# A table with a place in time for every step, in a decoder step of two layers on one core

## The chip, the core and the metric

The kernel runs on one core of a Trainium2 chip. A core has engines that run side by side, each its own queue of instructions strictly in order: TensorE (PE, matmuls and transposes), VectorE (DVE), ScalarE (ACT), GpSimd (POOL) and SyncE (SP, which here issues most DMAs). They tell each other by semaphores when something is ready. Matmuls write to PSUM, which has eight banks; everything else lies in SBUF. The metric is the device time of one execution in microseconds; lower is better.

## The reference

One inference step of a hybrid decoder with two layers, for a prompt of 512 tokens and for 8 samples of 8 tokens each. D = 1024, so 576 token columns in all.

```python
# layer 0: gated DeltaNet mixer
h = rms_norm(x) * (1 + scale) + shift                # scale, shift, gate = c @ ada_w + b
qkv, z, beta, a = split(h @ w_in)
qkv = silu(causal_conv(qkv))
o, state = gated_delta_rule(q, k, v, g, beta, s0)    # chunked, with a triangular inverse per chunk
x = x + gate * ((rms_norm(o) * silu(z)) @ w_out)
# shared keys and values
k, v = split(modulate(x) @ w_kv)                     # k: RMS norm per head, partial rotary
# layer 1: differential attention
q, z = split(modulate(x) @ w_in)
k_all, v_all = [cache pages, k], [cache pages, v]    # samples: 1024 past positions in 8 pages
p = softmax(q1 @ k1) - lam * softmax(q2 @ k2)
x = x + gate * ((rms_norm(p @ v_all) * silu(z)) @ w_out)
```

## The kernel before

**Products.** The large products keep 8 x 128 rows of weights and stream the 576 columns in two halves of 288. For float32 accuracy weights and activations are each split into a high and a low part (hi, lo: `whi`, `wlo`, `hhi`, `hlo`), and a product is three matmuls: hi x hi, hi x lo, lo x hi. 105 chunks of 128 output rows are made so. All other matmuls are plain float32.

**Stages.** `Opening` (0 to about 48 us) loads x and the first modulation weights, makes the norm and the first two chunks. The first layer follows (class `Weave`, to about 620 us): 8 groups of 2 heads, each with convolution, transposes, scaled keys, a triangular inverse in small blocks (`tinv_pe`: 32x32 and 64x64 parts of the PE array), the chain over 4 chunks, and the samples' states. 24 units of modulation weights (`ada_units`) run beside them with 128x32 parts of the array. Then the second layer (class `Second`): output projection of layer 0, second norm, q, k, v and gate products, the samples' attention over cache pages, the prompt's attention, the output projection.

**The order.** Nothing is ordered by hand. Each piece of work is a generator that yields its next step: the engine ("E" PE, "L" PE for small blocks, "A" ACT, "D" and "S" DVE, "P" and "Q" POOL, None for none), a cost in microseconds and conditions (names of results, `Room` for a free buffer). `drive` keeps a clock per engine, and at each turn runs the step that can start soonest; among those that can start at the same time, the one with the smallest key. The order in which steps are run is the order of the instructions in each engine's queue (`pin`, `woven`). The key before is a rank per work plus an entry of `NUDGE`, by the work's name and count: 188 entries for the first layer, 72 for the second. Once a work has its rank, all its steps have it.

The planner's prices: `matmul`, `turn` and, in the second layer, `change` add to a step's cost; a change of the array's shape costs 0.2 us back to 128x128 and 0.115 otherwise. `ready` adds `PAD` when a PE step follows another engine. DMA transfers get a landing time from `transfers`, with a margin per kind in `SLACK`. Where PE would be idle for over `GAP` = 0.6 us, `fill` issues dummy bf16 matmuls of 105 ns by its account (L368; in the opening L535), in the first layer alone; in the second it returns 0.

**The start.** In `body`, four records of matmuls on zeros (L3227), then a memset of part of `hhi` on POOL (L3228) and eight matmuls on it (L3230) run before `Opening`.

**Samples' attention.** `Sample2.keys` (one per sample b) builds block queries `qs`, and for each half of the sample's 8 key pages takes one of two `px` banks and makes the scores of 4 pages: 8 matmuls per page in 128x32 parts, for b >= `PB` = 3 four pages in one step (`BURST`), else two. ACT copies a half to SBUF (L2642). When both are done `softmax` starts: a PE step of its own makes the scores with the new keys in another `px` bank, 8 matmuls with 64 columns (all samples' new keys, of which 8 are this sample's), DVE adds the mask to the 8 columns that count, and max, exp and transposes follow. `values` makes the product with the value pages.

## Time and profile before

| | us |
|---|---|
| median of 3 runs | 1127.67 |
| lowest, highest | 1126.29, 1132.82 |
| the profiled execution, its own time | 1126.22 |
| its span, first to last instruction | 1124.5 |
| granted TensorE clock, mean | 0.995 |
| idle time of PE before steps that waited for POOL WF L868, ACT hhi L2785, DMA wlo<-wall, DVE hlo L1959 | 2.4, 2.2, 2.0, 2.0 |
| DMA, mean | 213 GB/s |

The profile is of one execution. Times within it are counted from the first instruction. A row of a group gives line, engine, operation, tiles (out<-in), shape and count, then busy time, mean duration and the idle time before it. A row of the timeline gives start, duration, engine, line, operation, tiles, shape and count. Matmuls overlap each other, so what one costs is read from start to start, not from its duration; a float32 matmul leaves two records, a transpose or a 288-column product one. Shapes like 128*32 are the rows and columns of the array in use. L347 and L2034 are the helpers that issue matmuls in the first and the second layer, so tiles tell what is what: pp and pq hold large products, px<-pg the scores with cache pages, px<-kT,qs those with the new keys, po<-pg the products with value pages, sc<-kT,qT the prompt's scores, pa<-araw modulation units.

### The profile page before, as it was taken

How to read it: one execution, taken by the hardware profiler on the slowest of the kernel's cores; microseconds unless marked ns; L12 is line 12 of the kernel's file. 1: busy time of each engine (PE TensorE's matmuls, PEld its weight loads, DVE VectorE, ACT ScalarE, POOL GpSimd, SP SyncE). 2: the span in 40 equal slices, each digit the busy share in tenths (PEclk: the TensorE clock that was granted, in tenths of full speed). 3: DMA queues.
4: the chain of work that ended last, by engine and by line, in shares of the span. 5: the costliest groups of instructions: out<-in, count | busy, mean ns of one | idle time of the engine just before them, and what ended most of it. 6: DMA issues, size and time to landing. Idle time of an engine off the chain costs nothing.

```text
span 1124.5 us, 32457 instructions
## 1 busy us (share of the span) xinstructions
PE 1098.5 (98%) x12641; PEld 1025.7 (91%) x12641; DVE 702.9 (63%) x1839; ACT 678.2 (60%) x1829; POOL 453.9 (40%) x769
## 2 busy tenths in 40 slices
PE   8989999999999999999999999999999999999998
PEld 6789999999999999999999899899898888888988
DVE  3576986878767887677835659574333457654421
ACT  3476867778596876868564334685444567655510
POOL 3434434344334433343124441589862233323421
PEclk8999999999999999999999999999999999999999
DMA  9685776584767766586696849413849888888742
GB/s 364 194 221 138 176 187 188 150 238 115 199 159 209 193 186 154 119 258 193 205 289 204 317 139 352 167 64 109 297 147 315 301 306 287 299 307 296 264 137 92
DMA packets 87643, 239.97 MB, mean 213 GB/s; under 512 B 14450, under 2 KB 28658, under 8 KB 87490
## 3 DMA queue, kind: packets, MB, share of 16 engines
q1 hardware_dynamic: 71938, 181.27, 46.6%
q0 software_dynamic: 15552, 56.63, 22.2%
q8 instruction: 100, 1.64, 0.6%
q14 instruction: 53, 0.43, 0.1%
HBM read 212.02 MB, written 25.84 MB: 212 GB/s over the span
## 4 chain that ended last, share of the span: by engine, by line
PE 88%; DVE 4%; DMA 3%; POOL 2%; issue 1%; ACT 1%; SPq 0%; POOLq 0%; DVEq 0%; ACTq 0%
PE pp L347 28%; PE pp L2034 14%; PE pq L2034 7%; PE pc L347 6%; PE px L2034 4%; PE po L2034 4%; PE pa L347 3%; PE sc L2034 3%; PE pt L2039 3%; PE pt L347 3%; PE ps L347 2%; PE pv L2034 2%; PE pt L2034 2%; PE pt L361 2%; PE pp L368 1%
## 5 line engine op out<-in xcount | busy, mean ns | idle before, releaser
L347 PE MATMUL pp<-hlo,whi 128*128 128x288 f32 x592 | 170.7, 310 | 0.0
L347 PE MATMUL pp<-hhi,whi 128*128 128x288 f32 x592 | 162.0, 295 | 0.0
L2136 POOL TENSOR_TENSOR wlo<-wraw,whi 128x512 fp32r<-128x512 f32 x78 | 104.2, 1350 | 110.8 <-ACT whi L2130 96.5
L2034 PE MATMUL pp<-hhi,whi 128*128 128x288 f32 x432 | 131.6, 305 | 0.0
L2034 PE MATMUL pp<-hlo,whi 128*128 128x288 f32 x432 | 127.3, 295 | 2.7 <-DVE hlo L1959 2.0
L2034 PE MATMUL pp<-hhi,wlo 128*128 128x288 f32 x432 | 126.8, 299 | 0.0
L347 PE MATMUL pp<-hhi,wraw 128*128 128x288 f32 x576 | 122.5, 298 | 0.0
L347 PEld LDWEIGHTS pp<-hlo,whi 128*128 128x128 f32 x592 | 111.5, 188 | 1.7 <-issue 1.0
L347 PEld LDWEIGHTS pp<-hhi,whi 128*128 128x128 f32 x592 | 111.5, 188 | 0.7
L347 PE MATMUL pp<-hhi,wlo 128*128 128x288 f32 x592 | 103.1, 303 | 2.0 <-DMA wlo<-wall 2.0
L347 PEld LDWEIGHTS pp<-hhi,wraw 128*128 128x128 f32 x576 | 93.6, 188 | 1.0 <-issue 0.2
L347 PEld LDWEIGHTS pp<-hhi,wlo 128*128 128x128 f32 x592 | 85.1, 188 | 3.6 <-DMA wlo<-wall 2.3
L1218 DVE SCALAR_TENSOR_TENSOR y<-u,vec,y 128x600 f32<-128x600 f32 x96 | 82.8, 868 | 5.0 <-ACT y L1215 4.0
L2034 PEld LDWEIGHTS pp<-hlo,whi 128*128 128x128 f32 x432 | 81.5, 189 | 3.1 <-DVE hlo L1959 2.2
L347 PE MATMUL pp<-hlo,wraw 128*128 128x288 f32 x288 | 84.1, 314 | 0.1
L2034 PEld LDWEIGHTS pp<-hhi,whi 128*128 128x128 f32 x432 | 81.4, 188 | 2.1 <-issue 1.8
L2034 PEld LDWEIGHTS pp<-hhi,wlo 128*128 128x128 f32 x432 | 81.8, 191 | 0.0
L2593 POOL COPY pg<-ptt 1x1 int32<-1x1 int32 x128 | 26.4, 217 | 122.4 <-PE po L2034 55.9
L1012 POOL DMA_DIRECT2D wlo<-wall x36 | 32.1, 893 | 94.3 <-ACT wlo L1007 65.9
L2130 ACT CAST whi<-wraw 128x1024 fp32r<-128x1024 f32 x45 | 47.2, 1048 | 35.7 <-PE px L2034 12.9
L2034 PE MATMUL pq<-hhi,whi 128*128 128x288 f32 x192 | 62.1, 324 | 0.2 <-ACT vch L2350 0.2
L2034 PE MATMUL pq<-hlo,whi 128*128 128x288 f32 x192 | 56.6, 295 | 0.0
(507 smaller groups left out, 3113.9 us busy)
## 6 DMA issues: line engine op xcount, KB each, us to landing
pg<-ck SPq DMA_DIRECT2D x64, 512.0 KB, 5.3
pg<-cv SPq DMA_DIRECT2D x64, 512.0 KB, 5.6
wraw<-wall SPq DMA_DIRECT2D x49, 512.0 KB, 4.3
wraw<-wall POOLq DMA_DIRECT2D x36, 512.0 KB, 7.0
whi<-wall POOLq DMA_DIRECT2D x36, 512.0 KB, 5.9
wlo<-wall POOLq DMA_DIRECT2D x36, 512.0 KB, 7.0
araw<-ada SPq DMA_DIRECT2D x24, 512.0 KB, 6.2
araw<-ada SPq DMA_DIRECT2D x8, 1024.0 KB, 13.5
```

Source lines behind the costliest of these rows:

```text
L347: return self.K.nc.tensor.matmul(**kw)
L361: return self.K.nc.tensor.transpose(**kw)
L368: self.K.nc.tensor.matmul(out=self.banks[0][:, HT:512].rearrange("p (a b) -> p a b", b=32), lhsT=self.K.ident[:, 0:64].bitcast(BF16), rhs= ...
L1012: K.nc.gpsimd.dma_start(out=lo[:], in_=src, accum_op=ALU.add)
L1218: nc.vector.scalar_tensor_tensor(out=y[:, :YW], in0=u[:, j:j + YW], scalar=cw[j], in1=y[:, :YW], op0=ALU.mult, op1=ALU.add)
L2034: return self.K.nc.tensor.matmul(**kw)
L2039: return self.K.nc.tensor.transpose(**kw)
L2130: nc.scalar.copy(out=hi[:], in_=raw[:])
L2136: (nc.vector if shared else nc.gpsimd).tensor_sub(out=lo[:, q:q + 4], in0=raw[:, q:q + 4], in1=hi[:, q:q + 4].bitcast(F32))
L2593: nc.gpsimd.tensor_copy(out=e, in_=P.ptt[0:1, i:i + 1])
```

## The change

1. `NUDGE` goes. `PLAN` holds, for each work, a place in time for each of its steps: 3435 steps of the first layer, 2274 of the second. A work is found by its name and a checksum of its path (the works that added it, with counts). The key of a step is its place; where there is none, `LAST` = 10000 plus the old rank. `Opening` has no table.
2. The planner's prices change: one rule for both layers, shape changes `ENTER` 0.23 (from 128x128), `ACROSS` 0.137 (between smaller shapes), `EXIT` 0.1 (back); small matmuls are counted per position in the array, the slowest position telling; `PAD` 0.5 to 0.1; `SLACK` of "w" 1.0 to 2.0 and of "x" 6.0 to 3.5 in the first layer.
3. For samples b >= `PB` the scores with the new keys are made in the step of the second half's pages, which takes both `px` banks and waits for all new keys. For all samples these matmuls have 8 columns instead of 64.
4. The memset of `hhi` and the eight matmuls behind it go from the start.
5. Opening a later tile of a group waits for ("cs0", g); the condition for choosing a free bank for gate products moves into `pick`.

```diff
-NUDGE = {
...
+PLAN = {
+    "Weave": """ada_loads 766088 14922 -11238 7264 2040 951 1320 2419 -702 1511 4123 2612 47 3127 3708 -1357 4500 3316 3411 975 1512 -624 -338 281 2685
...
+def planned(cls):
+    out = {}
+    for line in PLAN.get(cls, "").split("\n"):
+        name, i, *steps = line.split() or ("", 0)
+        at, out[name, int(i)] = 0, []
+        for t in steps:
+            at += int(t)
+            out[name, int(i)].append(at / 100)
+    return out
...
     def matmul(self, **kw):
...
+        if wide:
+            self.cost += 0.16 if rhs.dtype == BF16 else max(0.062, n * 0.00046)
+        elif shape == (128, 128):
+            self.cost += max(0.224, n * 0.00175)
         else:
-            cost = max(0.224, n * 0.00168)
...
+            at = kw.get("tile_position")
+            lane = self.lanes.get(at, 0.0) + max(0.062, n * 0.00182)
+            self.lanes[at] = lane
+            self.cost += max(0.0, lane - self.lane)
+            self.lane = max(lane, self.lane)
...
+    def turn(self, shape):
         if shape != self.shape:
-            self.cost += 0.2 if shape == (128, 128) else 0.115
-        elif kind == 2 and self.kind != 2:
-            self.cost += TURN
-        self.shape, self.kind = shape, kind
+            self.cost += EXIT if shape == (128, 128) else ENTER if self.shape == (128, 128) else ACROSS
...
+    def key(self, v):
+        return v[5][v[6]] if v[6] < len(v[5]) else LAST + v[0]
...
-PAD = 0.5
+PAD = 0.1
...
         for pair in range(4 // many):
             ids = [b * NPG + 4 * half + many * pair + i for i in range(many)]
-            yield "E", None, *[("kpage", i) for i in ids], *((Room("px"),) if pair == 0 else ())
+            joined = b >= PB and half
+            yield ("E", None, *[("kpage", i) for i in ids], *((Room("px"),) if pair == 0 else ()),
+                   *((Room("px"), *[("k", h) for h in range(8)]) if joined else ()))
...
+            if joined:
+                self.new(qs, W.took[1])
...
+    def new(self, qs, xr):
...
-                K.mm(out=pn[32 * j:32 * j + 32, 0:64], lhsT=qs[:, h, :], rhs=P.kT[:, h, SEQ:],
+                K.mm(out=pn[32 * j:32 * j + 32, 0:8], lhsT=qs[:, h, :], rhs=W.P.kT[:, h, SEQ + 8 * b:SEQ + 8 * b + 8],
                      start=(hh == 0), stop=(hh == 1), tile_position=(0, 32 * j))
...
+        if b < PB:
+            yield "E", None, Room("px"), *[("k", h) for h in range(8)]
+            self.new(qs, *W.took)
...
-                nc.gpsimd.memset(K.hhi[:, 0, 0:512].bitcast(F32), 0.0)
-                for n in (512, 512, 512, 512, 256, 256, 256, 256):
-                    nc.tensor.matmul(out=warm[:, 0:n], lhsT=K.hhi[:, 0, 0:128], rhs=K.hhi[:, 0, 0:n], start=True, stop=True)
```

## The prediction

> **What bounds the kernel now.** I read the page first, then the busy time by stage, then who PE (TensorE) waited for.

> ```profile
> span 1124.5 us, 32457 instructions
> PE 1098.5 (98%) x12641; PEld 1025.7 (91%) x12641; DVE 702.9 (63%) x1839; ACT 678.2 (60%) x1829; POOL 453.9 (40%) x769
> ...
> PE 88%; DVE 4%; DMA 3%; POOL 2%; issue 1%; ACT 1%; SPq 0%; POOLq 0%; DVEq 0%; ACTq 0%
> ```

> PE is busy 98% of the span and holds 88% of the chain that ended last; DVE and ACT are idle for over a third. So the time is PE's queue, and an order of steps is worth only what it takes out of that queue. Three things in it are not arithmetic: idle time, dummy matmuls, and changes of the array's shape.

> **Idle time, by stage** (start:end, length, busy time and instructions of each engine, granted clock, DMA share, GB/s):

> ```profile
> 0.00:48.00 48.00, 43.53 (x363) 33.29 (x364) 25.82 (x72) 21.46 (x45) 18.33 (x52) 0.93 0.89 310
> 48.00:620.00 572.00, 563.99 (x6638) 538.81 (x6637) 416.92 (x1132) 404.83 (x1188) 217.66 (x376) 1.00 0.70 188
> 620.00:700.00 80.00, 76.81 (x713) 74.32 (x712) 54.50 (x127) 29.92 (x58) 26.43 (x24) 0.98 0.75 263
> 700.00:800.00 100.00, 96.37 (x987) 92.28 (x989) 59.68 (x95) 65.00 (x125) 75.72 (x96) 1.00 0.42 148
> 800.00:1060.00 260.00, 259.35 (x3470) 229.89 (x3462) 125.87 (x365) 145.97 (x395) 97.70 (x209) 1.00 0.82 283
> 1060.00:1124.50 64.50, 58.41 (x489) 57.13 (x487) 20.09 (x51) 11.02 (x20) 18.02 (x14) 1.00 0.39 121
> ```

> PE is the first engine in each row. Its idle time: 4.5 us in the opening, 8.0 in the first layer (48 to 620), 3.2 up to 700, 3.6 up to 800, 0.65 up to 1060, 6.1 at the end. The opening moves 310 GB/s at a DMA share of 0.89 and has no entries in the table: nothing is to be had there.

> **Dummy matmuls.** Where the planner foresees a gap on PE over 0.6 us it fills it with `fill` (L368).

> ```profile
> L368 PE MATMUL pp<-cT,con_ident 128*128 128x224 bf16 x92 | 10.7, 260 | 0.0
> ```
> ```profile
> 537.86 1.60 PE L368 MATMUL pp<-cT,con_ident 128*128 128x224 bf16 x15
> 539.29 0.61 PE L347 MATMUL pc<-S,k 128*128 128x256 f32 x2
> ```

> The first row is the group in 48 to 620: 92 of them. In the timeline 15 take 539.29 - 537.86 = 1.43 us, 0.095 each, so 92 hold PE for 8.8 us. They count as busy, but they are foreseen idle time. With the 8.0 above, the first layer has 16.8 us in which PE does nothing useful.

> **Changes of shape.** Most matmuls use the whole 128x128 array. Scores, cache values, modulation and the small inverses use parts of it (128x32, 64x128, 32x32, 64x64). I call one unbroken stay in such a shape a visit.

> ```profile
> 1014.00 1.95 PE L2034 MATMUL px<-pg,qs 128*32 128x128 f32 x64
> 1015.88 0.40 PE L2034 MATMUL pq<-hhi,whi 128*128 128x288 f32 x1
> 1016.12 0.29 PE L2034 MATMUL pq<-hlo,whi 128*128 128x288 f32 x1
> 1016.25 0.29 PE L2034 MATMUL pq<-hhi,wlo 128*128 128x288 f32 x1
> ...
> 1017.44 0.29 PE L2034 MATMUL pq<-hhi,wlo 128*128 128x288 f32 x1
> 1017.66 0.43 PE L2034 MATMUL px<-kT,qs 128*32 128x64 f32 x16
> 1018.02 0.49 PE L2034 MATMUL pv<-vn,pts 128*128 128x128 f32 x2
> ```

> Start to start, a 288-column matmul takes 0.13 us in a row of its kind. The one before a visit takes 0.22 (1017.44 to 1017.66): +0.09. The one after takes 0.24 (1015.88 to 1016.12): +0.11. A visit of 64 records of 128 columns takes 1.88 (1014.00 to 1015.88), one of 16 records of 64 columns 0.36 (1017.66 to 1018.02). If half the columns cost half, 56 records make the difference of 1.52: 0.027 for one of 128 columns, and 1.88 - 64 x 0.027 = 0.14 beside the records. Together 0.34 us per visit that no arithmetic explains. From the code there are some 160 after the opening (24 modulation units, 8 samples and 48 inverse steps in the first layer; 12 modulation pairs, 22 for cache keys, 8 for new keys, 16 for cache values, 24 for prompt scores in the second): about 54 us.

> **The change part by part.** The sum is made against the profiled execution's own 1126.22 us (span 1124.5 and 1.7 around it); the median of the runs shown, 1127.67, lies 1.45 above.

> *Opening.* The memset of hhi and the 8 matmuls at L3230 go.

> ```profile
> 5.19 2.40 PE L3230 MATMUL ps<-hhi 128*128 128x512 f32 x8
> 7.43 2.86 PE L535 MATMUL ps<-WF 128*128 128x224 bf16 x28
> 10.12 3.88 PE L347 MATMUL pt<-ones,sq 128*128 128x1 f32 x30
> ...
> 16.76 1.94 PE L347 MATMUL pt<-araw,cT 128*32 128x256 f32 x16
> ...
> 21.85 1.07 PE L347 MATMUL pt<-araw,cT 128*32 128x256 f32 x16
> ```
> ```profile
> 12.90:19.70 6.80, 6.80 (x42) 4.71 (x42) 0.51 (x2) 0.94 (x2) 1.23 (x1) 0.50 1.02 412
> ```

> Behind them stand 28 fillers, and only at 10.12 the first real work, which needs DVE's sums of squares. 2.40 us fewer ahead of fillers move nothing: 0. What could cost is the clock: 0.50 between 12.9 and 19.7, where the same 16 matmuls take 1.94 instead of 1.07. If fewer matmuls lengthen that stretch by two such visits, +1.7 at most; if it moves away, -0.9. Inside the DMA-bound opening I take 0. [...]

> *Table, first layer.* 3435 steps get a place of their own instead of a rank per work with 188 nudges. 16.8 us are there to be taken. The waits behind the 8.0 are few and large, so orderable (the three largest; total, times, longest):

> ```profile
> PE pp L347 <- DMA wlo<-wall: 2.0, 1, 2.0
> PE pa L361 <- ACT adsb L202: 1.8, 1, 1.8
> PE pc L347 <- DVE r L1492: 1.4, 2, 1.1
> ```

> Each is a step that stood in PE's queue ahead of its input, which another order can mend.

> ```profile
> 528.00:542.00 14.00, 7.76 (x68) 6.15 (x68) 1.00 0.87 239
> ```

> But of L368 alone, 68 of the 92 fillers lie in these 14 us around the last group's inverse, where few products are left to put between; they go only if earlier products are held back, which needs their weights and banks. Bounds 0 and -16.8; I take half, **-8.4**.

> *The seam and the second layer.*

> ```profile
> PE px L2034 <- ACT hhi L2785: 2.2, 1, 2.2
> PE pp L2034 <- DVE hlo L1959: 2.0, 1, 2.0
> ...
> PE px L2034 <- DVE hlo L2787: 0.3, 1, 0.3
> ```
> ```profile
> 624.00:627.20 3.20, 3.20 (x27) 2.87 (x30) 2.77 (x2) 0.41 (x2) 3.20 (x3) 0.50 0.31 112
> ```

> At 620 PE waits 2.0 us for the last head's low part (L1959), and then runs 3.2 us at half clock, which costs 1.6. With the stage's 3.2 idle that is 4.8; half, **-2.4** (0 to -4.8). From 700 to 1060 4.3 idle; half, **-2.1** (0 to -4.3). At the end 2.6 of the 6.1 are the waits for L2785 and L2787, the rest is the drain of the last output; half of 2.6, **-1.3** (0 to -2.6).

> *New keys.* For the five samples from the fourth on, the visit for the new keys (16 records, 0.36 us) joins that of the last four pages: one visit's 0.34 saved each, -1.7. Its matmuls read 8 columns instead of 64. The 0.36 holds 0.36 - 0.14 = 0.22 for the records; between nothing and all of it I take half, 0.11 for each of 8 samples: -0.9. Together **-2.6** (-1.7 to -3.5). [...] No row here has an 8-column matmul in this shape. What the join costs: the step takes both px banks and waits for all keys (k). Behind it on PE stand the gate products (pq); if the second bank isn't free, they wait for an ACT copy of 0.59 us:

> ```profile
> L2642 ACT COPY sp<-px 128x512 f32<-128x512 f32 x16 | 9.4, 586 | 11.7 <-PE px L2034 11.7
> ```

> Five times that is +2.9. The planner knows the bank and puts pq products ahead; I take 0.

> *Fewer visits elsewhere.* The planner's price of a change of shape was 0.115 in and 0.2 out; it is now 0.23 and 0.1, and 0.137 between two small shapes, and the narrow matmuls are counted by position. So orders that put a modulation unit beside a sample's or an inverse's visit now look cheaper. Bounds 0 and, if 30 of 160 join, -10; I take 15, **-5.1**.

> *Less slack.* PAD, what the planner adds when a PE step follows another engine, falls from 0.5 to 0.1 us, and weights are taken to land 1 us later (SLACK "w"), x 2.5 us sooner. So PE steps are placed up to 0.4 us closer behind ACT and DVE, and PE takes its queue strictly in order: one late step holds all behind it. Before, with 0.5, only some twenty of about 600 such steps were late. I take 20 more by 0.2: **+4** (0 to +40, see below).

> SP and POOL: page loads, weights and modulation loads keep their number; their issue moves with the table. SP's waits are for buffers, and the planner counts the two queues as before, so I give this nothing beside the rival on DMA. `pick`'s condition moves inside the function and chooses the same bank; ("cs0", g) repeats what the first tile of a group waited for already: 0.

> Sum: -8.4 - 2.4 - 2.1 - 1.3 - 2.6 - 5.1 + 4 = -17.9, so 1126.2 - 17.9 = **1108**.

> **Rivals.** *Nearly all of it goes:* all idle time and fillers that can go (16.8 + 4.8 + 4.3 + 2.6), 30 visits (10) and the new keys (2.6) less the 4: -37, 1089. For it: DVE and ACT have room. Against: the tail of the first layer.

> *DMA takes the second layer's place:* from 800 to 1060 the share is already 0.82 at 283 GB/s, and page buffers are few, so saved PE time turns into waits for pages. Then only the first layer's -8.4, half of the visits (-2.6) and the opening count, against +4 to +8: 1119 to 1123. Against: no row of PE's waits names a page.

> *Slower, by less slack:* if of the 600 PE steps behind another engine a third lose 0.2 us each, that is +40 instead of +4, and 1126 - 22 + 40 = 1144. It decides from 22/600 = 0.037 us a step on. For it: one late r (L1492) held all of PE's queue for 1.1. Against: the handful of waits now, and that the products put between are 0.13 us each, fine enough to fill such gaps.

> *The table doesn't fit:* places are looked up by a checksum of each work's path; a miss falls back to LAST + rank, the old rank without nudges, worth at most what those gave. The names in the table are those of the works; I hold it for unlikely and count it with no change: 1126 give or take 5.

> **How the numbers follow.** Forecast (1100 to 1117) 0.60; nearly all goes (below 1100) 0.15; DMA or no fit (1117 to 1131) 0.15; less slack (above) 0.10. Some 0.5% (5.6 us) is what a measurement can tell here: of the third case 0.04 falls below 1120.6. Faster 0.79, same 0.11, slower 0.10. The range reaches from just under the second case, 1088, to 1126; above it lie the slower case and part of the third, below it little.

> **What would show it.** In the profile after: L368 in the first layer under 50 (right) or near 92 (wrong); PE's idle time from 48 to 620 about 4 to 6 us; no or a shorter half-clock stretch near 620; px<-kT,qs with 8 columns and five fewer stays; PE waits by ACT and DVE in small pieces under 0.5 us, some 4 us more of them (much more: the slack rival); waits for pg<-ck or pg<-cv would be the DMA rival. If idle and fillers fall but the span doesn't, visits or waits took their place and the halves I chose are wrong.

## The result, and the profile after

The kernel after takes 1116.47 us (median of four runs, 1113.36 to 1117.56) against 1127.05 before (also four runs): ratio 0.9891, 95% interval 0.9851 to 0.993. The forecast was 1108 with a range from 1088 to 1126. Direction and range held; 10.6 us were gained by the medians, 12.3 by the ratio, where 18 were forecast. The profiled execution took 1117.56, its span is 1115.6.

First the page of the kernel after, then its busy time by the stages of before (the first engine in each row is PE):

```profile
span 1115.6 us, 32355 instructions
PE 1093.1 (98%) x12604; PEld 1025.0 (92%) x12604; DVE 688.8 (62%) x1839; ACT 677.1 (61%) x1829; POOL 459.4 (41%) x768
```
```profile
0.00:48.00 48.00, 43.52 (x351) 32.40 (x352) 26.42 (x74) 22.32 (x46) 19.97 (x55) 0.93 0.86 302
48.00:620.00 572.00, 563.47 (x6606) 538.43 (x6604) 407.27 (x1127) 401.10 (x1186) 220.53 (x370) 0.99 0.70 189
620.00:700.00 80.00, 75.37 (x780) 73.02 (x779) 48.05 (x121) 30.43 (x60) 26.94 (x26) 0.98 0.80 266
700.00:800.00 100.00, 99.94 (x944) 98.27 (x944) 59.88 (x102) 66.10 (x128) 74.98 (x94) 1.00 0.40 134
800.00:1060.00 260.00, 258.71 (x3539) 231.04 (x3537) 133.23 (x379) 150.73 (x407) 101.49 (x212) 1.00 0.85 293
1060.00:1115.60 55.60, 52.11 (x396) 51.81 (x394) 13.97 (x38) 6.39 (x7) 15.47 (x13) 0.99 0.36 115
```

PE's idle time in the first layer did not fall: 572.00 - 563.47 = 8.5 us, where it was 8.0. Around the seam (620 to 700) it rose from 3.2 to 4.6. Behind that it went: 3.6 to 0.06 from 700 to 800, and 6.1 to 3.5 at the end. From 800 to 1060 it is 1.3 (0.65 before).

PE's waits after (total, times, longest) say what the idle time is:

```profile
PE pp L1087 <- DVE hlo L2709: 4.1, 1, 4.1
PE pa L1087 <- DMA araw<-ada: 2.7, 1, 2.7
PE ps L1087 <- DVE Ss L2669: 2.6, 2, 1.9
PE ps L3958 <- POOL WF L1616: 2.4, 1, 2.4
PE pp L1087 <- DMA wlo<-wall: 1.5, 1, 1.5
```

Three of the five are longer than before; the wait for L2785 at the end is gone. The first is the seam's: 4.1 us for a low part, where it was 2.0. The second is at the first layer's start. There the timeline of PE shows this:

```profile
45.25 4.95 PE L1108 MATMUL pp<-cT,con_ident 128*128 128x224 bf16 x50 [1.04 <-DVE v L1527]
52.86 1.04 PE L1087 MATMUL pa<-araw,cT 128*32 128x128 f32 x16 [2.67 <-DMA araw<-ada]
53.84 0.61 PE L1087 MATMUL pp<-hlo,whi 128*128 128x288 f32 x1
```

Fifty dummy matmuls, then 2.67 us without work, and only then the first product at 53.84. Before, 12 dummies ran from 46.57, and the products began at 47.65:

```profile
46.57 1.31 PE L368 MATMUL pp<-cT,con_ident 128*128 128x224 bf16 x12 [1.04 <-DVE v L779]
47.65 0.38 PE L347 MATMUL pp<-hlo,whi 128*128 128x288 f32 x1
```

So the first layer begins 6.2 us later. The dummies as a whole, each from 44 to 620 us, before (L368) and after (L1108):

```profile
L368 PE MATMUL pp<-cT,con_ident 128*128 128x224 bf16 x104 | 12.0, 260 | 1.0 <-DVE v L779 1.0
```
```profile
L1108 PE MATMUL pp<-cT,con_ident 128*128 128x224 bf16 x93 | 9.9, 259 | 1.0 <-DVE v L1527 1.0
...
L1108 PE MATMUL pp<-cT,con_ident 128*128 128x224 bf16 x16 | 1.9, 260 | 0.0
```

The last row is the same view from 525 to 545 us, around the last group's inverse: 16, where there were 68. The start took 38 more. And the clock has a share. After the opening there are three stretches of 3.4 us at half clock, where before had one (623.9 to 627.3), and at a clock of 0.50 each costs, by estimate, half of that, some 1.7:

```profile
517.20:520.60 3.40, 3.40 (x17) 3.38 (x16) 2.67 (x9) 0.93 (x5) 0.00 (x0) 0.50 1.03 244
626.40:629.80 3.40, 3.40 (x17) 3.40 (x15) 0.00 (x0) 0.00 (x0) 1.94 (x2) 0.50 0.60 181
53.00:56.40 3.40, 3.40 (x27) 3.02 (x23) 1.37 (x3) 1.32 (x2) 0.81 (x3) 0.50 0.32 43
```

These stretches are not the same in every execution. Of the four runs of after the profiled one is the slowest (1117.56, mean clock 0.992); the fastest took 1113.36 at 0.995. And the run keys_undone (below), whose PE queue is that of after through the whole first layer, has no stretch near 53 (its mean clock is 0.995).

One number sorts it out. Both traces have 5024 matmuls of 288 columns. I number them from 0 in order of their starts; the start of one in the trace of after less that of the same number before shows where the kernel gains: -1.3 us at number 79 (the opening's last), +6.2 at 80 (the first layer's first), -4.4 at 2500, +0.8 at 2640, +1.0 at 2719 (the first layer's last), +4.6 at 3000, -1.5 at 3300, -8.9 at the last. The first layer gains some 10 us on the way and gives it all back at its two ends; the second layer has the whole result.

### The profile page after: what moved, and what is told of

It is laid out like the page before. It is cut to its first block, busy times and chain, and to the rows that moved or that the text cites. A ratio compares the mean times of both kernels' runs of the same rounds, so it can differ in the third digit from the quotient of the medians.

```text
span 1115.6 us, 32355 instructions
## 1 busy us (share of the span) xinstructions
PE 1093.1 (98%) x12604; PEld 1025.0 (92%) x12604; DVE 688.8 (62%) x1839; ACT 677.1 (61%) x1829; POOL 459.4 (41%) x768
## 3 DMA queue, kind: packets, MB, share of 16 engines
q8 instruction: 99, 1.62, 0.6%
## 5 line engine op out<-in xcount | busy, mean ns | idle before, releaser
L1087 PE MATMUL pp<-hlo,whi 128*128 128x288 f32 x1024 | 302.6, 307 | 4.1 <-DVE hlo L2709 4.1
L1968 DVE SCALAR_TENSOR_TENSOR y<-u,vec,y 128x600 f32<-128x600 f32 x96 | 84.2, 883 | 10.1 <-ACT y L1965 9.4
L3313 POOL COPY pg<-ptt 1x1 int32<-1x1 int32 x128 | 29.0, 237 | 114.2 <-issue 44.6
L1087 PE MATMUL pq<-hhi,wlo 128*128 128x288 f32 x200 | 59.0, 295 | 0.0
L1087 PE MATMUL pq<-hlo,whi 128*128 128x288 f32 x200 | 59.0, 295 | 0.0
L1087 PEld LDWEIGHTS pp<-hlo,wraw 128*128 128x128 f32 x288 | 54.2, 188 | 1.8 <-issue 1.0
L2659 POOL TENSOR_TENSOR wm<-w,con_mask 96x512 fp32r<-96x512 f32 x32 | 35.3, 1102 | 46.9 <-PE ps L1087 46.8
L3563 ACT ACTIVATE pm<-sc,mx 128x128 f32<-128x128 f32 (+3 forms) x64 | 33.7, 528 | 23.9 <-DVE mx L3558 22.8
L2669 DVE SCALAR_TENSOR_TENSOR Ss<-Ss,egl,ps 128x128 f32<-128x128 f32 x128 | 40.1, 340 | 12.9 <-PE ps L1087 12.4
L1761 POOL DMA_DIRECT2D wraw<-wall x18 | 15.9, 882 | 74.0 <-ACT wraw L1756 48.0
```

The source lines that it names most:

```text
L1087: return self.K.nc.tensor.matmul(**kw)
L1761: K.nc.gpsimd.dma_start(out=lo[:], in_=src, accum_op=ALU.add)
L1968: nc.vector.scalar_tensor_tensor(out=y[:, :YW], in0=u[:, j:j + YW], scalar=cw[j], in1=y[:, :YW], op0=ALU.mult, op1=ALU.add)
L2659: nc.gpsimd.tensor_mul(out=wm[:], in0=s.w3[:, hh, a, :].bitcast(F32).unsqueeze(1).to_broadcast([96, 4, 128]), in1=K.smaskb.unsqueeze(2).to ...
L2669: nc.vector.scalar_tensor_tensor(out=s_, in0=s_, scalar=s.egl[:, hh, 4 + 4 * a + b:5 + 4 * a + b], in1=ps[:, b, :], op0=ALU.mult, op1=ALU.add)
L3313: nc.gpsimd.tensor_copy(out=e, in_=P.ptt[0:1, i:i + 1])
```

## The experiments

The planner can't be asked to change one thing: any price or wait moves thousands of steps. So most kernels here have the order of one or both layers written out as a list of steps (with their dummies), as the planner had made it, and `drive` takes the next of the list whatever its clock says. A list as the planner made it leaves every queue as it was.

```diff
+    def listed(self):
...
+        return self.live if self.now_at is None else [v for v in self.live if v[7] == self.now_at[0]]
...
-            for v in self.live:
+            for v in self.listed():
```

Times are compared as ratios to runs of the kernel before on the same chip, whose median was 1127.24 to 1127.58.

**One layer's order at a time.** The kernel before with the first layer's list of after:

> The kernel before, with the first layer's steps (and dummies) put in the order that they have after; opening and second layer in the order of before. Theory (the first layer is even, the gain is the second layer's): 1127 + 1, so 1126 to 1130. Rival, the prediction's split: -8.4 for the idle time and fillers and some -2 for joined stays, 1115 to 1119.

Measured 1130.94, ratio 1.0025 (1.0009 to 1.0041): slower by 2.8 us, a little above the range that the theory gave. And the kernel after with the first layer's list of before:

> The kernel after, with the first layer's steps (and dummies) put in the order that they have before, and no wait for the group's conv state ahead of the later tiles. Theory: the whole gain is kept, 1127 - 11 to - 13, so 1114 to 1116.5. Rival, the prediction's split (second layer -2.4 - 2.1 - 1.3 - 2.6 and half of the joined stays, against +4 of less slack): -7 or less, 1120 and more.

Measured 1115.7, ratio 0.9891 (0.9867 to 0.9915): the same ratio as the whole change. The two settle it. As it stands, the first layer's table is worth nothing or a little less, and the second layer's order (with the new-key scores) is worth all 12 us.

From 288-column product number 2750 to the last, the kernel before takes 495.8 us and this one 482.6. Counted in the two traces over that stretch, PE's idle time falls from 8.0 to 1.8 (-6.2), and the stays in smaller shapes from 69 to 58. At the prediction's 0.34 each that is -3.7. Half clock falls from 2.4 us to none (-1.2). With the narrower scores (below, some -0.9) this makes -12.0 of the -13.2. The -1.2 isn't the order's work: PE's wait of 2.0 us ahead of that stretch stands in both traces.

**The start of the first layer.** In the list of after, the first unit is moved and 38 dummies go:

```diff
 first layer, list of steps
-ada_units1 step 0, 50 dummies ahead of it
 projections1 open1
-projections1 steps 1 to 9
+projections1 steps 1 to 9, 12 dummies ahead of them
+ada_units1 step 0
```

> The kernel after, with the order of every engine kept as it is and two things moved back to where they stand before: 12 dummy matmuls instead of 50 ahead of the first layer's first product, and the first modulation unit behind some 30 products instead of ahead of them. Theory (the first layer's gain was spent at its start): 38 dummies of 0.1 us, 2.7 us of waiting for araw and some 1.7 us of half clock go, 6 to 7 us, 1116.5 becomes 1110 (1109 to 1112). Rival (the late start costs nothing, because something later in the layer, a weight set or another engine, sets the pace: after was 6.2 us behind before at the layer's first products and only 1.0 behind by product 1500): within 2 us of 1116.5.

Measured 1113.25, ratio 0.9863 (0.9838 to 0.9888), 3.2 us under after and about half of what was expected; the intervals of the two overlap, the profiled spans (1111.5 and 1115.6) differ by 4.1. The products did begin 6.6 us earlier and the half clock near 53 is gone (as it is in keys_undone without this edit); from 55.46 to 55.59 a 288-column matmul takes 0.13 from start to start. But the wait for araw stayed, since the load, too, landed 1.8 us later than after (52.86 there). The row of this kernel:

```profile
54.65 0.64 PE L1095 MATMUL pa<-araw,cT 128*32 128x128 f32 x16 [2.40 <-DMA araw<-ada]
```

So the unit has to stand further back still (run best2 does that). At product number 300, 2.1 of the 6.6 us are gone again, since the unit with its wait now stands behind the first products instead of ahead of them; 4.1 are left at the last. The rival, by which the late start costs nothing, falls by the traces.

**DVE held up by POOL.** In the kernel after, the wait of 1.9 us for Ss near 605 us has this ahead of it (timeline of DVE and POOL):

```profile
601.75 1.04 POOL L2659 TENSOR_TENSOR wm<-w,con_mask 96x512 fp32r<-96x512 f32 x1 [1.77 <-PE ps L1087]
602.09 3.27 DVE L2689 TENSOR_TENSOR y<-u,rst 128x64 f32<-128x64 f32 x1
602.75 2.53 POOL L1803 TENSOR_TENSOR wlo<-ckq,whi 128x512 fp32r<-128x512 f32 x2
605.29 0.33 DVE L2263 SCALAR_TENSOR_TENSOR S<-S,egl,pc 128x128 f32<-128x128 f32 x1
```

L2689 is an addition of 64 columns, which takes 0.23 at its median. It begins while POOL is at a multiplication (601.75 to 602.79) and ends just behind POOL's two subtractions (602.75 to 605.28); the state updates stand behind it in DVE's queue. Of the 24 instructions at L2689 in this trace five took more than 0.23 us; each began while POOL was at an elementwise operation and ended 0.08 to 0.09 us behind the end of one. The edit puts the eviction that ends in L2689 behind them:

```diff
 first layer, list of steps
-projections1 evac74 (D)
 chunks8 chain1, sample8 sample_states2 (D)
+projections1 evac74 (D)
```

> The kernel after with one edit: on DVE the eviction of an output tile near 602 us, whose last addition took 3.27 us beside POOL's 2.53, goes behind the state updates that PE waits for. Theory (the addition was held up by POOL's two subtractions, and PE's wait of 1.93 us hung on it): the addition takes 0.23 in its new place, the wait falls under 0.5, 1116.5 - 1.9, about 1114.6 (1113.5 to 1115.5). Rival (DVE is simply late there, or the state updates are held up instead): the wait stays, 1116 to 1117.

Measured 1113.66, ratio 0.9874 (0.9853 to 0.9896): 1.9 less than after by the ratios, 2.8 by the medians, in line with -1.9 though the interval overlaps that of after. The rows are clearer. Of PE's two waits for Ss, 2.6 in all, the one of 1.9 is gone and 0.7 is left. The same addition in its new place:

```profile
602.30 2.54 POOL L1822 TENSOR_TENSOR wlo<-ckq,whi 128x512 fp32r<-128x512 f32 x2
602.56 0.86 DVE L2688 SCALAR_TENSOR_TENSOR Ss<-Ss,egl,ps 128x128 f32<-128x128 f32 x3
603.33 0.44 DVE L2702 SCALAR_TENSOR_TENSOR y<-pp,mod,u 128x224 f32<-128x224 f32 x1
603.69 0.21 DVE L2706 TENSOR_TENSOR rst<-pp,mod 128x64 f32<-128x64 f32 x1
603.94 0.99 DVE L2708 TENSOR_TENSOR y<-u,rst 128x64 f32<-128x64 f32 x1
```

The updates, which read PSUM, run at their own pace beside POOL (0.86 us for three); the addition, with both inputs in SBUF, is still held (0.99, not the 0.23 expected), but nobody on PE waits for it.

**The seam.** PE's 4.1 us are for low parts of the last heads; on DVE they stood behind the eviction of the last output tile, and that behind a held-up L2401 (1.30 us instead of 0.45). The second layer's products of these heads carry no condition on them in the code, so the planner doesn't see them late.

```diff
 first layer, list of steps
+projections1 out_head13, out_head12 (low parts, DVE)
 post8 head2, head1 (low parts, DVE)
-projections1 evac78 (D)
...
-projections1 out_head13, out_head12 (low parts, DVE)
+projections1 evac78 (D)
```

> The kernel after with the second of these two edits alone: on DVE the low parts of the last heads ahead of the eviction of the last output tile. PE's order is untouched. Theory: PE's wait of 4.13 us for the last low part falls to 2 or less and the half clock of 626.4 to 629.8 goes or not: 1116.5 - 2 to - 4, so 1112.5 to 1114.5. Rival: the wait goes over to the weights' low part that POOL splits at the same time: 1116 to 1117.

Measured 1111.12, ratio 0.9857 (0.983 to 0.9884): 3.8 less than after by the ratios, 5.3 by the medians; the intervals overlap. The wait for the low part is gone altogether, and in the trace the half clock behind it too (288 columns take 0.13 from start to start there, 626.22 to 626.36): 4.1 + 1.7. What comes up in its place is half as long:

```profile
625.81 0.44 PE L1109 MATMUL pt<-con_ident,scr 128*128 128x128 f32 x2 [2.23 <-ACT scr L3743]
```

That copy (L3743, 0.36 us on ACT) stood behind a weight cast which itself had to wait.

**All three, and two more.** The three edits together:

> The kernel of the run start (50 dummies back to 12, the first modulation unit behind the first products), and on DVE two groups of steps in another order: near 602 us the eviction of an output tile (its last addition took 3.27 us instead of 0.23 while POOL worked for 2.53) goes behind the state updates that PE waited 1.93 us for; near 621 us the last two heads' low parts go ahead of the evictions, since PE waited 4.13 us for them. Theory: start's 1113.3 less 1.9 less 1.5 to 2, and less another 1.7 if the half-clock stretch behind the seam goes too: 1108 (1106.5 to 1110). Rival: other inputs are late right behind these two (weights that POOL splits, loads), so that PE waits for them instead: 1112 to 1114.

Measured 1107.32, ratio 0.9822 (0.9799 to 0.9846). Then the first unit three PE steps later, and the small copy ahead of the weight cast on ACT:

```diff
 lists of steps
-ada_units1 step 0, behind projections1 step 9
+ada_units1 step 0, behind projections1 step 12
...
-weights1 split_w2 (A), ahead of ada_mod1 (A)
+weights1 split_w2 (A), behind ada_mod1 (A)
```

> The kernel of the run best1 with two more moves: the first modulation unit another three of PE's steps later (PE waited 0.97 us for its araw there), and on ACT the small copy of the modulation's result ahead of the second weight set's cast, behind which it stood while PE waited 2.23 us for it. Theory: 1107.3 - 0.9 - 2, 1104.5 (1103 to 1106). Rival: both waits only hide others that end at the same time: 1106.5 to 1108.

Measured 1103.38, ratio 0.9783 (0.9761 to 0.9805): faster than both kernels, 24 us under before and 12 to 13 under after. Its longest waits after the opening:

```profile
PE pp L1095 <- DMA wlo<-wall: 1.1, 1, 1.1
PE pp L1095 <- ACT u L1941: 1.1, 2, 0.6
```

In its trace the clock is full from 16.4 us to the last product. From the opening's last 288-column product (number 79) to the first layer's last (2719) it takes 567.4 us, where the kernel before took 572.4 and the kernel after 574.7.

**The scores with the new keys.** Undone in the kernel after, its order otherwise kept:

```diff
-                joined = b >= PB and half
+                joined = False
...
-        if b < PB:
+        if True:
...
-                K.mm(out=pn[32 * j:32 * j + 32, 0:8], lhsT=qs[:, h, :], rhs=W.P.kT[:, h, SEQ + 8 * b:SEQ + 8 * b + 8],
+                K.mm(out=pn[32 * j:32 * j + 32, 0:64], lhsT=qs[:, h, :], rhs=W.P.kT[:, h, SEQ:],
```

> The kernel after, with the scores of the new keys as they were: 64 columns wide, and for the last five samples in a stay of their own, two of PE's steps behind the last pages; the rest of the order untouched. The prediction's term: +2.6 (1.7 to 3.5), so 1119. By the rows of the two profiles (a stay of its own with 64 columns 0.36, with 8 columns 0.24, joined 2.01 against 1.88 without, 0.20 for the way in and out) +2.7. Rival (what the stays save is lost in the softmax, which begins later or waits for the second bank): 0 to -1.

Measured 1118.22, ratio 0.992 (0.9897 to 0.9943) against 0.9891: +3.3 by the ratios, +1.8 by the medians, in agreement, though the intervals overlap. From 288-column product number 2750 to the last, the two traces take 485.8 and 483.3 us: +2.5. The rows carry the point. In the kernel after, a stay of its own and a joined one:

```profile
834.69 0.31 PE L1087 MATMUL px<-kT,qs 128*32 128x8 f32 x16
834.93 0.40 PE L1087 MATMUL pp<-hhi,whi 128*128 128x288 f32 x1
...
877.80 0.31 PE L1087 MATMUL px<-kT,qs 128*32 128x8 f32 x16
877.95 1.93 PE L1087 MATMUL px<-pg,qs 128*32 128x128 f32 x64
879.82 0.38 PE L1087 MATMUL pv<-vn,pts 128*128 128x128 f32 x1
```

Start to start, the stay of 8 columns takes 834.93 - 834.69 = 0.24, where that of 64 columns took 0.36. The joined stay takes 879.82 - 877.80 = 2.02, where the pages alone took 1.88: a joined sample pays 0.14 instead of 0.36 and the 0.09 + 0.11 of the way in and out. In after and with the part undone alike, the order leaves the new keys of two of the first three samples beside a stay for cache values. With 64 columns one of them is:

```profile
851.23 0.43 PE L1095 MATMUL px<-kT,qs 128*32 128x64 f32 x16
851.48 1.93 PE L1095 MATMUL po<-pg,pTs 128*32 128x128 f32 x64
853.34 0.44 PE L1109 MATMUL pt<-con_ident,vch 128*128 128x128 f32 x2
```

853.34 - 851.23 = 2.11. The same stay in the kernel after, with 8 columns, starts at 853.85, and the transposes behind it at 855.87: 2.02. The narrowing is worth some 0.1 inside a longer stay as well.

**The warm-up** taken from the kernel before:

> The kernel before without the memset and the 8 warm-up matmuls of the opening, nothing else. The prediction's 0: 1127 within 0.7. Rival by the clock (the start at half clock gets longer): +1.7, 1128.7. Rival by the trace of after, whose first layer product came 0.5 to 0.8 us earlier: 1126.3.

Measured 1128.76, ratio 1.0005 (0.999 to 1.002): no effect clear of noise, as forecast. The interval reaches from -1 to +2 us, so the times don't exclude the clock rival's +1.7. Its mechanism doesn't show: the half clock of the opening lasted 3.4 us instead of 6.8, and the first layer's first product came 0.4 us earlier. Two other stretches, near 75 and 1081 us, came up that the profile of before hasn't. Over the twelve runs of this kernel, all with one order, the mean clock goes from 0.991 to 0.997, so such stretches come and go with an order unchanged.

**No table**, with the new prices and the joined scores kept:

```diff
-PLAN = {
...
+PLAN = {}
```

> The kernel after with an empty table: every step falls back to its work's old rank, without the old nudges; the new prices, PAD and the joined scores stay. Theory (the places found by search carry the gain): slower than before, by 1 to 4 per cent, since the nudges are gone as well: 1138 to 1170. Rival (the prices carry it, the table little): 1113 to 1122.

Measured 1157.03, ratio 1.0264 (1.0238 to 1.0291). The prices alone, with bare ranks, are 41 us slower than with the table. It says nothing of prices with the old nudges, which this kernel doesn't have either.

## Why the prediction was right, and where its steps failed

- **What bounds the kernel** was right: PE's queue. In the kernel after none of PE's waits is for a page, so the rival on DMA falls. (In the other runs the longest such wait of PE is 1.3 us, in no_table; in keys_undone there is one of 0.2.) That the table doesn't fit falls too, since no_table is 41 us slower.
- **First layer, -8.4: failed as it stands.** The idle time rose by 0.5 where it was to fall to 4 to 6 us, the dummies from 44 us on went from 104 to 93, and first_only is 2.8 us slower. The choice of "half" wasn't the fault: of the tail's 68 dummies, which the prediction doubted most, 52 went. What failed is another line, the one that gave ("cs0", g) a cost of 0. In the code, opening the first later tile now waits for the group's conv state, and the planner starts a chunk's products only when its tile is open; so it sees no product for 5.5 us (LATENCY 2.3, 0.2 for the load, SLACK 3.0), fills with 50 dummies, and lets the first unit in ahead. On the chip the products could begin at 47.65, as they did before. That this wait is the reason is read from the code; the run start moved the dummies and the unit, it didn't keep the planner and take the wait alone. Beside it stands what the prediction had no term for: DVE held by POOL (1.9) and two stretches of half clock (by estimate some 1.7 each in the profiled execution). With the start and the DVE order mended and no half clock (best2), the layer is 5.0 shorter than before, counted from the opening's last product.
- **Seam, -2.4: wrong sign.** The wait grew from 2.0 to 4.1 and the half clock behind it stayed. The run seam shows that an order can take the wait away: 3.8 by the ratios, of a bound of 4.8. The table is made on the planner's clock, which has no condition there by the code.
- **700 to 1060, -2.1, and the end, -1.3: right, and under-sized.** Idle time fell by 3.6 - 0.06 + 0.65 - 1.3 = 2.9 and by 6.1 - 3.5 = 2.6; the two waits at the end went wholly. (The stages are cut at the same times in both, while after runs some 9 us ahead at the end; from product number 2750 to the last the idle time falls from 8.0 to 1.8.)
- **New keys, -2.6: right.** By the rows a stay of its own with 64 columns cost 0.36 + 0.20 = 0.56. Five joined samples save 0.56 - 0.14 = 0.42 each, three others 0.12 by fewer columns: -2.5. The narrowing, taken as 0.11 from half of 0.22, measures 0.36 - 0.24 = 0.12, for 16 records spread over four positions of the array.
- **Fewer visits elsewhere, -5.1: half of it.** The traces have 76 + 69 = 145 stays before, where the prediction counted some 160. In the first layer there are 77 after (matmuls of 96 rows counted with the whole array), so none were joined. In the second there are 11 fewer (58), 4 of them by the join (62 in keys_undone), so 7 elsewhere: 7 x 0.34 = 2.4.
- **Less slack, +4: didn't come.** From 48 us on PE waited 14.2 us in 19 waits for ACT and DVE before and 10.1 in 10 after. Those of at most 0.5 us fell from 3.4 us in all to 1.5. A PAD of 0.1 with a search behind it is no looser than 0.5; the slower rival falls with it.
- **Opening, 0: right.** no_warm_up shows no loss clear of noise (ratio 1.0005, 0.999 to 1.002).

Without the first layer's -8.4, 2.7 of the visits and the +4, -17.9 becomes -10.8, beside the 10.6 measured. That this fits so well is luck in part: the sum still holds -2.4 for the seam, where PE in fact waited 2.1 us longer, and the idle time behind the seam, put at -3.4, fell by 5.5. And that the forecast itself lay in the right range is owed to a wide range and to errors of both signs: the largest term, the first layer's, gave nothing, and the loss of 4 didn't come. The second layer is where the prediction's mechanism held. Without the seam its terms (-2.1, -1.3, -2.6 and half of the visits, -2.6) make -8.6, and second_only, which has the seam of before, gained 11.9.

## What to carry to other kernels

An order found by search is as good as the clock that it is found on. Where a planner has a wait too many (a tile's opening) or one too few (the last heads' low parts), or doesn't know that one engine holds up another (here POOL made an addition on DVE take 3.27 us instead of 0.23), the search puts the loss right there, and it shows as one long wait or a block of dummies. Freeze the order as a list, move those few steps by hand, and look at the next wait: here five such moves were worth about as much as the whole change (12.2 and 12.3 us by the ratios).

## What the runs showed of the hardware

**POOL holds up DVE.** An addition of 64 columns on DVE, with both inputs in SBUF, took 3.27 us instead of 0.23: it waited out the rest of one POOL operation and two more of 2.53 together, while DVE's updates from PSUM ran on unhindered once they stood ahead of it (0.86 us for three, in state_order). In the trace of after the 33 updates of Ss that lay wholly within a POOL operation on tensors took 0.34 us at the median, the 65 beside none as much. What it is in the two kinds of operation that makes the difference, no run tried.

```profile
70.92:74.33 3.41, 1.62 (x13) 1.38 (x11) 2.46 (x9) 2.07 (x4) 0.81 (x3) 1.00 1.05 262
...
620.49:623.90 3.41, 1.41 (x11) 1.27 (x10) 3.20 (x7) 1.31 (x2) 1.62 (x2) 1.00 0.76 257
```

and from the kernel after:

```profile
513.80:517.21 3.41, 1.92 (x74) 1.70 (x74) 3.25 (x6) 3.27 (x12) 3.22 (x3) 0.99 1.03 337
49.55:52.96 3.41, 0.74 (x11) 0.52 (x13) 2.01 (x3) 2.06 (x5) 0.29 (x3) 1.00 0.42 144
...
602.50:605.95 3.45, 2.63 (x21) 2.40 (x19) 3.45 (x4) 1.18 (x5) 2.78 (x3) 1.00 0.47 152
605.95:609.36 3.41, 2.30 (x17) 2.29 (x18) 2.75 (x11) 0.00 (x0) 1.58 (x2) 1.00 0.85 263
```

Behind 0.74, 1.41 and 1.92 of 3.41 the clock fell to half (64 of the 74 matmuls in the 1.92 were 32x32 pieces); behind 1.62 it didn't. The Ss wait of 1.93 us fell across two grid steps, left 2.63 and 2.30 in them, and cost no clock. So one stall of 2 us cost 2, and another, the 2.0 at the seam of before, by estimate 3.7 (2.0 and half of 3.4). PE's busy time isn't the whole of it, though: in the opening of before the clock fell at 12.90 behind a grid step in which PE was busy throughout, from 10.12 on with matmuls of a single column:

```profile
9.49:12.90 3.41, 3.41 (x35) 3.41 (x32) 1.86 (x3) 0.91 (x2) 0.00 (x0) 1.00 1.04 399
```

These are few cases. If PE's busy time in such a step decides, which is the author's reading of them, 1.41 (fell) and 1.62 (didn't) put the limit for whole-array matmuls near 1.5 of 3.41, as an estimate; how small shapes or single columns count was not tried.
